# A two-layer encoder trunk on one core: start addresses of the split activations and blocks, 32-bit scores, and two block slots fewer

## The chip, the cores and the metric

The kernel runs on 1 core of a Trainium2 chip. The metric is device microseconds from start to end of one execution; a median over several runs stands for a kernel. The engines are TensorE (PE, with its weight loads shown apart as PEld), VectorE (DVE), ScalarE (ACT), GpSimd (POOL) and SyncE (SP), which issues the transfers.

## The reference: what is computed

Two sequences of 256 tokens (512 rows together), width 1024, go through two layers. Each layer is a mixer and a gated FFN with a three-tap convolution over tokens:

```python
h = rms_norm(x, norm_mix[i])
# layer 0: differential attention, 8 heads, two score maps per head, heads of 64
a = softmax(q0 k0) - lam * softmax(q1 k1);  o = a @ v;  o = rms_norm(o)
# layer 1: three dilated window groups of 8 heads of 64, joined by their log-sum-exp
# both layers: 4 heads of 64 of cross-attention into 256 memory tokens
x = x + concat([mixed, cross]) @ w_out
x = x + (silu(a) * b) @ w_down,   a, b = conv3(rms_norm(x) @ w_up)
```

q and k of every attention are normalised per head and, but for the cross-attention, rotated on 16 of their 64 elements.

## The kernel before

**Products.** A float32 operand of a large product is held as two parts, a high part rounded to the 32-bit form fp32r and a low part (the rest). `mm3` (L370 to L374) makes one product of three matmuls: high by high (L371), then the two mixed ones (L372, L373). In the trace a matmul's tiles are written out<-moving,stationary. In the QKV projections the activations `hh`, `hl` are stationary and the weights `wh`, `wl` move; in the FFN's up-projection the weights are stationary and `hh`, `hl` move; in the down-projection and the output projection the activations lie in block slots (`blk`) and are stationary.

**Storage.** `hh` and `hl` are [128, 8, 512] fp32r tiles. `blk` is a pool of 30 slots of 128 x 512 elements; a `Slots` object gives out the slot that comes free first. Slots hold gains and memory tokens as they land, q and k blocks, v, the split outputs of attention and the split FFN activations (20 slots in the first of the three FFN parts, 16 in the second, 8 in the third). Before the last FFN part of layer 0, `mem_tiles` loads and normalises the memory tokens of layer 1 into slots while the second part's are still held.

**Scores.** `qk_post` (L599) normalises, rotates and transposes q or k. `block_evac` (L572) then takes a block of two heads (64 partitions each) from its PSUM bank. For kind "-" one ACT instruction (L575) makes one float32 block. For kinds "q" and "k" two ACT instructions (L582) write the high parts of the two heads to two blocks, and two DVE instructions (L587) the low parts; for q the low part lies in the other 64 partitions of the same block, for k in a third block, and two more DVE copies (L594) repeat k's high part. So a matmul over 128 partitions (L833) gives high by high plus low by high, and one over 64 partitions (L835) adds high by low. Blocks of kind "-" are multiplied as plain float32 over 64 partitions (L840); there are two heads, on partitions 0 to 63 and 64 to 127. All scores over 256 keys are of the first sort (L833, L835); in layer 1 the two groups over 128 keys are of the second (L840). Each float32 matmul appears as two MATMUL records.

A score group is what `scores` (L827) issues for one tile of 128 tokens: two pieces of 256 keys in layer 0's mixer (4 head pairs x 4 tiles = 16 groups) and in the cross-attention (2 layers x 4 tiles = 8 groups), one piece of 256 and two of 128 in layer 1's mixer (16 groups).

**Order.** The order of all instructions is worked out while the kernel is built: generators run against a small model of the engines (`Sched`, with costs such as `c_act`, `c_dve`, `c_mm`), and whichever part is due next writes its instructions. Attention work is thus laid between the projections' matmuls. Weights come as 220 units of 512 KB through `raw` slots on SP's queue, are split by ACT (L348) and DVE (L350), and are held in 6 slots of `wh` and `wl`.

Of the kernel before, what the change touches and what calls it, by code (L numbers as in the profile page):

```python
# [21 lines left out]
NTOK = 512  # L22
# [5 lines left out]
LAM_INIT = 0.8 - 0.6 * math.exp(0.0)  # L28
BIG = 1e30
QS = -0.125  # L30
N_BLK, N_W = 30, 6
X0_U, X1_U = 1, 3
FIRST = [(0, 0), (1, 0), (0, 1), (1, 1), (2, 0), (2, 1), (0, 2), (1, 2), (2, 2), (3, 0), (3, 1), (3, 2), (0, 3), (1, 3), (2, 3), (3, 3)]
X_AT = (1, 2, 3)
# [5 lines left out]
class Event:  # L40
    def __init__(self, sched):
        self.s, self.t, self.waiters, self.val = sched, None, [], None
# [51 lines left out]
class Slots:  # L94


    def __init__(self, sched, pool, name, n, shape):
        self.s, self.pool, self.name, self.shape = sched, pool, name, shape
        self.free = [(0.0, i) for i in range(n)]
        self.waiters = deque()  # L100

    def get(self, dt=F32):
        if self.free:
            j = min(range(len(self.free)), key=lambda i: self.free[i])
            t, i = self.free.pop(j)
            if t > self.s.now:
                yield t
        else:
            e = self.s.event()
            self.waiters.append(e)  # L110
            yield e
            i = e.val
        v = self.pool.tile(self.shape, dt, tag=f"{self.name}{i}", bufs=1, name=f"{self.name}{i}")
        return Slot(self, i, v)

    def put(self, i, t):
        if self.waiters:
# [144 lines left out]
def trunk_kernel(ctx: ExitStack, tc: tile.TileContext, io: dict, out: bass.AP):  # L262
# [6 lines left out]
    small = ctx.enter_context(tc.tile_pool(name="small", bufs=6))  # L269
    psum = ctx.enter_context(tc.tile_pool(name="psum", bufs=1, space=bass.MemoryType.PSUM))  # L270

    def slots(name, n, shape=(128, 512)):
        return Slots(S, pool, name, n, list(shape))

    blk = slots("blk", N_BLK)
    e_s = slots("e", 3)
    eT_s = slots("eT", 3)
    on_s = slots("on", 1)
# [154 lines left out]
            tp.done(t)  # L433
        yield t

    hh = const.tile([128, KD, NTOK], F32R, name="hh")
    hl = const.tile([128, KD, NTOK], F32R, name="hl")

    def norm_h(t, gkey, permuted, x_ev, h_ev):

# [105 lines left out]
            if all((u, x) == (u, t) or FIRST.index((u, x)) < FIRST.index((u, t)) for x in range(NT)):  # L546
                ws[u][2](S.free["PE"])

    class QBlock:


        def __init__(self, a):
            self.a = a

        def done(self, t):
            for x in self.a:
                x.done(t)

    class KBlock:


        def __init__(self, a, lo):
            self.a, self.lo = a, lo

        def done(self, t):
            for x in self.a + [self.lo]:
                x.done(t)

    def half(h):
        return slice(64 * h, 64 * h + 64)  # L570

    def block_evac(kind, bufs, tp, g):  # L572

        if kind == "-":
            nc.scalar.activation(bufs[0].v, tp.v, AF.Copy, scale=g)  # L575
            t = S.op("ACT", c_act(512, 1))
            yield t
            tp.done(t)
            return bufs[0]
        for h in range(2):  # L580
            pr = half(h)
            nc.scalar.activation(bufs[h].v[pr], tp.v[pr], AF.Copy, scale=g[pr])  # L582
            yield S.op("ACT", c_act(512, 1))
        for h in range(2):
            pr, po = half(h), half(1 - h)
            lo = bufs[2].v[pr] if kind == "k" else bufs[h].v[po]
            nc.vector.scalar_tensor_tensor(lo, tp.v[pr], g[pr], bufs[h].v[pr].bitcast(F32), ALU.mult, ALU.subtract)  # L587
            t = S.op("DVE", c_dve(512, 1))
        tp.done(t)
        yield t  # L590
        if kind == "q":
            return QBlock(bufs)
        for h in range(2):
            nc.vector.tensor_copy(bufs[h].v[half(1 - h)], bufs[h].v[half(h)].bitcast(F32))  # L594
            t = S.op("DVE", c_dve(512, 0, True))
        yield t
        return KBlock(bufs[0:2], bufs[2])

    def qk_post(rope, gcol, kinds, ev):  # L599

        qns = [None] * 2
        evs = [S.event() for _ in range(NT)]
# [1 line left out]
        def post(t, ps, done):  # L604
# [37 lines left out]
            if t == NT - 1:  # L642
                for e in evs:
                    yield e
                dst = []
                for b in range(2):
                    bufs = []
                    for _ in range({"-": 1, "q": 2, "k": 3}[kinds[b]]):
                        d = yield from blk.get(F32 if kinds[b] == "-" else F32R)
                        bufs.append(d)  # L650
                    tp = yield from tp_s.get()
                    for x in range(NT):
                        src = qns[x // 2].val.v.rearrange("p (t c) -> p t c", t=2)
                        nc.tensor.transpose(tp.v[:, x * 128:x * 128 + 128], src[:, x % 2, b * 128:b * 128 + 128],  # L654
                                            ident)
                        te = S.op("PE", T_PE)
                    yield te
                    d = yield from block_evac(kinds[b], bufs, tp, gcol[b])
                    dst.append(d)
                for q in qns:  # L660
                    q.val.done(te)
                ev.set(S.now, dst)
# [164 lines left out]
    def scores(sc, parts):  # L827

        for c, q, tq, k, ks in parts:
            n = ks.stop - ks.start  # L830
            if isinstance(q, QBlock):
                for h in range(2):
                    nc.tensor.matmul(sc[h].v[:, c:c + n], q.a[h].v[:, tq], k.a[h].v[:, ks], start=True, stop=False)  # L833
                for h in range(2):
                    nc.tensor.matmul(sc[h].v[:, c:c + n], q.a[h].v[half(h), tq], k.lo.v[half(h), ks],  # L835
                                     start=False, stop=True)
                t = S.op("PE", 4 * c_mm(n))
            else:
                for h in range(2):
                    nc.tensor.matmul(sc[h].v[:, c:c + n], q.v[half(h), tq], k.v[half(h), ks], start=True, stop=True)  # L840
                    t = S.op("PE", c_mm(n, True))
        return t

    def take(slots_, ev):
# [536 lines left out]
    def main():  # L1381
        ev = S.event

        xq, mk, mv = ev(), ev(), ev()
        cross = [ev(), ev()]
        mT = [ev() for _ in range(NT)]
        halves = [qk_post(None, gc(G_XQ[0], G_XQ[0]), "qq", xq)]
        outs = []
        for p in range(4):
            q, k, v = ev(), ev(), ev()  # L1390
            halves += [qk_post(ropes["aq"], gc(G_AQ, G_AQ), "qq", q), qk_post(ropes["ak"], gc(G_AK, G_AK), "kk", k), v_post(v)]
            res = [ev(), ev()]
            outs.append(res)
            S.spawn(attn_a(q, k, v, res))
        yield from proj_first("a_w_in", halves[0:2], h0)
        S.spawn(mem_tiles(0, mT))
        yield from proj("a_w_in", halves[2:4])
        S.spawn(attn_cross(xq, mk, mv, False, cross))
        a_outs = {"c": cross, **{str(i): x for i, x in enumerate(outs)}}
        for st in A_STEPS:  # L1400
            if st[0] == "M":
                yield from mem_proj(0, mT, [qk_post(None, gc(G_XK[0], G_XK[0]), "kk", mk), v_post(mv)])
            elif st[0] == "P":
                yield from proj("a_w_in", [halves[1 + 3 * int(n) + "qkv".index(x)] for x, n in st[1:]])
            else:
                yield from out_proj("a_w_out", a_outs[st[1]], None)
        x1 = [ev() for _ in range(NT)]
        h1 = norm_all("f0", io["norm_ffn"][0], False, x1)
        yield from out_proj_last("a_w_out", [a_outs[x] for x in A_LAST], x1)
        x2 = [ev() for _ in range(NT)]  # L1410
        mT = [ev() for _ in range(NT)]
        xq, mk, mv = ev(), ev(), ev()
        h2 = norm_all("h1", io["norm_mix"][1], True, x2, mv)
        yield from ffn(0, h1, x2, mT, [qk_post(None, gc(G_XK[1], G_XK[1]), "kk", mk), v_post(mv)])

        cross = [ev(), ev()]
        halves = [qk_post(None, gc(G_XQ[1], G_XQ[1]), "qq", xq)]
        S.spawn(attn_cross(xq, mk, mv, True, cross))
        outs = []
        for p in range(4):  # L1420
            q01, q2k0, k12, v01 = ev(), ev(), ev(), ev()
            halves += [qk_post(ropes["b0"], gc(G_BQ[0], G_BQ[1]), "q-", q01), qk_post(ropes["b1"], gc(G_BQ[2], G_BK[0]), "-k", q2k0),
                       qk_post(ropes["b2"], gc(G_BK[1], G_BK[2]), "--", k12), v_post(v01)]
            if p % 2 == 0:
                v2 = ev()
                halves.append(v_post(v2))
            res = ev()
            outs.append(res)
            S.spawn(attn_b(q01, q2k0, k12, v01, v2, (p % 2) * 128, p % 2 == 1, res))
        for i in range(0, len(halves), 2):  # L1430
            yield from proj("b_w_in", halves[i:i + 2], h2 if i == 0 else None, True)
        yield from out_proj("b_w_out", outs[0:2], None)
        x3 = [ev() for _ in range(NT)]
        h3 = norm_all("f1", io["norm_ffn"][1], False, x3)
        yield from out_proj_last("b_w_out", [cross, outs[2:4]], x3)
        yield from ffn(1, h3, None)
# [70 lines left out]
```

## Time and profile before

| | |
|---|---|
| median of 3 runs | 1434.92 us (1434.71 to 1435.49) |
| the profiled execution, its own time | 1434.02 us |
| its span in the trace | 1432.2 us |
| PE busy | 1402.8 us, 98% of the span |
| PEld busy | 1171.2 us |
| DVE, ACT, POOL busy | 841.1, 644.5, 338.4 us |
| chain that ended last | PE 87%, POOL 5%, DVE 3% |

The span runs from the first to the last instruction; what lies around it is 1.8 us. A matmul's shown duration is its modelled stay in the array and overlaps the next one's, so how fast PE goes is read from the distance between starts, or from how many matmuls fit in a stretch, not from the duration.

### The profile page before, as it was taken

What the parts mean: (1) busy time and instruction counts of PE and PEld (TensorE: products, weight loads), DVE (VectorE), ACT (ScalarE), POOL (GpSimd) and SP (SyncE); (2) the same over time, 40 slices, a digit from 0 to 9 for tenths busy, and PEclk for the clock granted to TensorE, in tenths of its full rate; (3) what the DMA queues carried; (4) which work ended last, traced back from release to release, by engine and by line L of the source; (5) the groups of instructions that cost most, each with busy time, mean ns of one, the idle gap of its engine ahead of it and who ended that gap; (6) DMA issues with size and microseconds to landing.
All of it is one profiled execution on the core that took longest, in us unless ns stands there. A gap on an engine that the chain in (4) does not pass through costs nothing.

```text
span 1432.2 us, 19017 instructions
## 1 busy us (share of the span) xinstructions
PE 1402.8 (98%) x7168; PEld 1171.2 (82%) x7168; DVE 841.1 (59%) x1314; ACT 644.5 (45%) x1177; POOL 338.4 (24%) x652
## 2 busy tenths in 40 slices
PE   6999999999999999999999999999999999999999
PEld 4778888879888888878878888888889888888887
DVE  5687778886664356546666444444476663466353
ACT  5666656535443144344446434444554442243231
POOL 5836554121000000030154155545130000000000
PEclk9999999999999999999999999999999999999999
DMA  6431131122333333433231222212223333323321
GB/s 224 156 97 50 33 110 60 60 74 89 118 95 97 101 90 103 114 122 121 73 93 53 72 70 66 60 60 74 88 78 100 103 89 102 94 98 103 89 74 59
DMA packets 39260, 129.33 MB, mean 90 GB/s; under 512 B 4608, under 2 KB 5504, under 8 KB 39168
## 3 DMA queue, kind: packets, MB, share of 16 engines
q1 hardware_dynamic: 39168, 128.11, 28.9%
q8 instruction: 57, 0.93, 0.3%
q14 instruction: 35, 0.29, 0.1%
HBM read 126.00 MB, written 2.10 MB: 89 GB/s over the span
## 4 chain that ended last, share of the span: by engine, by line
PE 87%; POOL 5%; DVE 3%; issue 2%; DMA 1%; ACT 1%; SPq 0%; POOLq 0%; DVEq 0%; ACTq 0%
PE acc L371 17%; PE acc L373 17%; PE acc L372 17%; PE sc L373 7%; PE sc L371 7%; PE sc L372 7%; PE tp L755 2%; POOL rstd L620 2%; PE o L1038 2%; PE sc L835 1%; PE sc L833 1%; PE tp L654 1%; PE tp L415 1%; PE o L371 1%; PE o L372 1%
## 5 line engine op out<-in xcount | busy, mean ns | idle before, releaser
L350 DVE TENSOR_TENSOR wl<-raw,wh 128x1024 fp32r<-128x1024 f32 x220 | 273.4, 1246 | 239.2 <-ACT wh L348 238.4
L348 ACT CAST wh<-raw 128x1024 fp32r<-128x1024 f32 x220 | 231.9, 1055 | 357.6 <-PE sc L372 182.3
L371 PE MATMUL acc<-wh,hh 128*128 128x512 f32 (+1 forms) x536 | 217.0, 405 | 0.6 <-ACT hh L428 0.6
L373 PE MATMUL acc<-wh,hl 128*128 128x512 f32 (+1 forms) x536 | 203.5, 380 | 0.0
L372 PE MATMUL acc<-wl,hh 128*128 128x512 f32 (+1 forms) x536 | 203.1, 379 | 0.0
L371 PE MATMUL acc<-wh,blk 128*128 128x512 f32 x368 | 148.9, 405 | 0.0
L372 PE MATMUL acc<-wl,blk 128*128 128x512 f32 x368 | 143.6, 390 | 0.0
L373 PE MATMUL acc<-wh,blk 128*128 128x512 f32 x368 | 143.5, 390 | 0.0
L371 PE MATMUL acc<-hh,wh 128*128 128x512 f32 (+1 forms) x384 | 143.1, 373 | 0.0
L371 PE MATMUL sc<-hh,wh 128*128 128x512 f32 (+1 forms) x384 | 142.9, 372 | 0.0
L373 PE MATMUL acc<-hh,wl 128*128 128x512 f32 (+1 forms) x384 | 142.6, 371 | 0.0
L373 PE MATMUL sc<-hh,wl 128*128 128x512 f32 (+1 forms) x384 | 142.6, 371 | 0.0
L372 PE MATMUL acc<-hl,wh 128*128 128x512 f32 (+1 forms) x384 | 142.6, 371 | 0.0
L372 PE MATMUL sc<-hl,wh 128*128 128x512 f32 (+1 forms) x384 | 142.6, 371 | 0.0
L373 PEld LDWEIGHTS acc<-wh,hl 128*128 128x128 f32 x536 | 101.1, 189 | 19.9 <-DVE hl L430 0.3
L371 PEld LDWEIGHTS acc<-wh,hh 128*128 128x128 f32 x536 | 101.8, 190 | 16.7 <-ACT hh L428 1.0
L372 PEld LDWEIGHTS acc<-wl,hh 128*128 128x128 f32 x536 | 101.7, 190 | 13.9 <-DVE wl L350 0.5
L386 POOL TENSOR_SCALAR s<-ss 128x1 f32<-128x1 f32 x24 | 11.4, 477 | 427.7 <-ACT qn L381 422.1
L620 POOL TENSOR_TENSOR rstd<-ss,mhalf 128x4 f32<-128x4 f32 x96 | 106.2, 1107 | 8.0
L373 PEld LDWEIGHTS acc<-hh,wl 128*128 128x128 f32 x384 | 72.3, 188 | 12.5
L372 PEld LDWEIGHTS acc<-hl,wh 128*128 128x128 f32 x384 | 72.3, 188 | 12.5
L373 PEld LDWEIGHTS sc<-hh,wl 128*128 128x128 f32 x384 | 72.3, 188 | 12.5
(152 smaller groups left out, 2486.7 us busy)
## 6 DMA issues: line engine op xcount, KB each, us to landing
raw<-w SPq DMA_DIRECT2D x220, 512.0 KB, 3.6
blk<-mem SPq DMA_DIRECT2D x16, 256.0 KB, 6.6
y<-X SPq DMA_DIRECT2D x8, 256.0 KB, 2.0
X<-x SPq DMA_DIRECT2D x3, 512.0 KB, 9.0
blk<-norm_mix SPq DMA_DIRECT2D x4, 256.0 KB, 6.3
blk<-norm_mem SPq DMA_DIRECT2D x4, 256.0 KB, 6.0
blk<-norm_ffn SPq DMA_DIRECT2D x4, 256.0 KB, 5.3
X<-x SPq DMA_DIRECT2D x2, 256.0 KB, 3.0
```

Of the source, the lines that this page charges most:

```text
L348: nc.scalar.copy(hi.v, r.v)
L350: nc.vector.tensor_tensor(lo.v, r.v, hi.v.bitcast(F32), ALU.subtract)
L371: nc.tensor.matmul(out_, ah, bh, start=start, stop=False)
L372: nc.tensor.matmul(out_, ah, bl, start=False, stop=False)
L373: nc.tensor.matmul(out_, al, bh, start=False, stop=stop)
L415: nc.tensor.transpose(tp.v[:, k * 128:k * 128 + 128], h[j].v[:, k * 128:k * 128 + 128], ident_)
L620: nc.gpsimd.tensor_tensor(rstd, ss, mhalf[:, 0:4], ALU.pow)
L654: nc.tensor.transpose(tp.v[:, x * 128:x * 128 + 128], src[:, x % 2, b * 128:b * 128 + 128], ident)
L755: nc.tensor.transpose(tp.v[:, i * 128:i * 128 + 128], e.v[:, i * 128:i * 128 + 128], ident)
L833: nc.tensor.matmul(sc[h].v[:, c:c + n], q.a[h].v[:, tq], k.a[h].v[:, ks], start=True, stop=False)
L835: nc.tensor.matmul(sc[h].v[:, c:c + n], q.a[h].v[half(h), tq], k.lo.v[half(h), ks], start=False, stop=True)
L1038: nc.tensor.matmul(o[:, t, h, :], eT.v[:, i * 128:i * 128 + 128], vt[s].v[:, c:c + 64], start=(i == 0), stop=(i == 3))
```

## The change

Four edits. (1) `hh` and `hl` get 16 elements more and begin 4 and 12 elements (16 and 48 bytes) into their tiles. (2) Each block slot gets 16 elements more, and slot i begins i mod 16 elements (0, 4 ... 60 bytes) into its tile. (3) All blocks of q and k are plain float32: `block_evac`, `QBlock` and `KBlock` are gone, every block is taken from PSUM by one ACT instruction, and every score is a float32 matmul over 64 partitions; the model's cost of such a pair of matmuls is counted once for the two heads. (4) 28 block slots in place of 30.

```diff
-N_BLK, N_W = 30, 6
+N_BLK, N_W = 28, 6
...
+        at = i * self.phase % 16
+        shape = [self.shape[0], self.shape[1] + (16 if self.phase else 0)]
+        v = self.pool.tile(shape, dt, tag=f"{self.name}{i}", bufs=1, name=f"{self.name}{i}")
+        return Slot(self, i, v[:, at:at + self.shape[1]])
...
-    blk = slots("blk", N_BLK)
+    blk = slots("blk", N_BLK, phase=1)
...
-    hh = const.tile([128, KD, NTOK], F32R, name="hh")
-    hl = const.tile([128, KD, NTOK], F32R, name="hl")
+    hht = const.tile([128, KD * NTOK + 16], F32R, name="hh")
+    hlt = const.tile([128, KD * NTOK + 16], F32R, name="hl")
+    hh = hht[:, 4:4 + KD * NTOK].rearrange("p (k t) -> p k t", k=KD)
+    hl = hlt[:, 12:12 + KD * NTOK].rearrange("p (k t) -> p k t", k=KD)
...
-                    bufs = []
-                    for _ in range({"-": 1, "q": 2, "k": 3}[kinds[b]]):
-                        d = yield from blk.get(F32 if kinds[b] == "-" else F32R)
-                        bufs.append(d)
+                    d = yield from blk.get()
+                    dst.append(d)
...
-                    d = yield from block_evac(kinds[b], bufs, tp, gcol[b])
-                    dst.append(d)
+                    nc.scalar.activation(d.v, tp.v, AF.Copy, scale=gcol[b])
+                    tp.done(S.op("ACT", c_act(512, 1)))
+                    yield S.free["ACT"] + S.LAT
...
-            if isinstance(q, QBlock):
-                for h in range(2):
-                    nc.tensor.matmul(sc[h].v[:, c:c + n], q.a[h].v[:, tq], k.a[h].v[:, ks], start=True, stop=False)
-                for h in range(2):
-                    nc.tensor.matmul(sc[h].v[:, c:c + n], q.a[h].v[half(h), tq], k.lo.v[half(h), ks],
-                                     start=False, stop=True)
-                t = S.op("PE", 4 * c_mm(n))
-            else:
-                for h in range(2):
-                    nc.tensor.matmul(sc[h].v[:, c:c + n], q.v[half(h), tq], k.v[half(h), ks], start=True, stop=True)
-                    t = S.op("PE", c_mm(n, True))
+            for h in range(2):
+                nc.tensor.matmul(sc[h].v[:, c:c + n], q.v[half(h), tq], k.v[half(h), ks], start=True, stop=True)
+            t = S.op("PE", c_mm(n, True))
```

The calls of `qk_post` lose their kinds ("qq", "kk", "q-", "-k", "--").

## Rows read from the trace of the kernel before

**Rows 1.** The page, busy time of the engines, share of the span, instructions.

```profile
PE 1402.8 (98%) x7168; PEld 1171.2 (82%) x7168; DVE 841.1 (59%) x1314; ACT 644.5 (45%) x1177; POOL 338.4 (24%) x652
```

**Rows 2.** Waits of PE over the span: engine, line, releaser: us, times, longest.

```profile
PE tp L415 <- DMA ident<-c_ident: 8.2, 1, 8.2
PE tp L415 <- DVE qn L403: 5.2, 7, 1.4
PE tp L654 <- POOL qn L639: 3.7, 3, 1.9
...
PE tp L415 <- DVE blk L587: 0.6, 1, 0.6
...
PE tp L654 <- DVE blk L587: 0.5, 1, 0.5
```

**Rows 3.** Windows: an attention stretch and an FFN stretch; busy us and counts.

```profile
100.00:200.00 100.00, 100.00 (x558) 82.06 (x557) 78.83 (x171) 61.55 (x163) 52.07 (x116) 1.00 0.21 61
...
400.00:500.00 100.00, 100.00 (x443) 82.84 (x442) 47.42 (x55) 29.87 (x36) 0.00 (x0) 1.00 0.32 96
```

**Rows 4.** Timeline of PE at 332 us: start, us, engine, line, tiles, shapes.

```profile
332.01 0.28 PE L373 MATMUL sc<-hh,wl 128*128 128x256 f32 x1
...
332.37 0.28 PE L373 MATMUL sc<-hh,wl 128*128 128x256 f32 x1
```

**Rows 5.** Timeline of PE, one score group of layer 0 and its successor.

```profile
126.00 0.40 PE L833 MATMUL sc<-blk,blk 128*128 128x256 f32 x2
...
126.63 0.50 PE L833 MATMUL sc<-blk,blk 128*128 128x256 f32 x2
...
127.38 0.50 PE L371 MATMUL acc<-wh,hh 128*128 128x512 f32 x1
```

**Rows 6.** Timeline of PE, a layer 1 group; its L840 also cut short.

```profile
800.59 0.40 PE L833 MATMUL sc<-blk,blk 128*128 128x256 f32 x2
800.91 0.38 PE L835 MATMUL sc<-blk,blk 64*128 64x256 f32 x2
801.13 0.61 PE L840 MATMUL sc<-blk,blk 64*128 64x128 f32 x8
801.67 0.50 PE L371 MATMUL acc<-wh,hh 128*128 128x512 f32 x1
...
801.13 0.27 PE L840 MATMUL sc<-blk,blk 64*128 64x128 f32 x2
```

**Rows 7.** Groups by line and shape, ACT and DVE: the blocks taken from PSUM.

```profile
L582 ACT ACTIVATE blk<-tp,gcols 64x512 fp32r<-64x512 f32 x64 | 43.6, 684 | 27.9 <-PE tp L654 27.3
L575 ACT ACTIVATE blk<-tp,gcols 128x512 f32<-128x512 f32 x16 | 11.1, 693 | 7.9 <-PE tp L654 7.8
L587 DVE SCALAR_TENSOR_TENSOR blk<-tp,gcols,blk 64x512 fp32r<-64x512 f32 x64 | 47.9, 749 | 23.0 <-ACT blk L582 22.2
L594 DVE CAST blk<-blk 64x512 fp32r<-64x512 f32 x32 | 13.5, 423 | 0.7
```

**Rows 8.** Groups by line: products that move `hh`, and loads from `hh` and `blk`.

```profile
L371 PE MATMUL acc<-hh,wh 128*128 128x512 f32 (+1 forms) x384 | 143.1, 373 | 0.0
L371 PEld LDWEIGHTS acc<-wh,hh 128*128 128x128 f32 x536 | 101.8, 190 | 16.7 <-ACT hh L428 1.0
L371 PEld LDWEIGHTS acc<-wh,blk 128*128 128x128 f32 x368 | 69.2, 188 | 12.6
L371 PEld LDWEIGHTS sc<-wh,blk 128*128 128x128 f32 x104 | 19.5, 188 | 4.0
L371 PEld LDWEIGHTS o<-wh,blk 128*128 128x128 f32 x72 | 13.5, 188 | 2.8
```

**Rows 9.** Groups by line and shape, DVE: output begins 4 bytes later, or not.

```profile
L1156 DVE SCALAR_TENSOR_TENSOR eT<-sc,convT,eT 128x510 f32<-128x510 f32 x44 | 32.9, 749 | 2.8 <-ACT eT L1151 2.8
L1158 DVE SCALAR_TENSOR_TENSOR eT<-sc,convT,eT 128x510 f32<-128x510 f32 x44 | 32.9, 749 | 1.6
```

**Rows 10.** Transfers into block slots: count, KB each, us to landing.

```profile
blk<-mem SPq DMA_DIRECT2D x16, 256.0 KB, 6.6
```

More of the change, by code (lines that the diff above doesn't have):

```diff
@@ L94, with __init__ @@
 class Slots:
-    def __init__(self, sched, pool, name, n, shape):
-        self.s, self.pool, self.name, self.shape = sched, pool, name, shape
+    def __init__(self, sched, pool, name, n, shape, phase=0):
+        self.s, self.pool, self.name, self.shape, self.phase = sched, pool, name, shape, phase
         self.free = [(0.0, i) for i in range(n)]
@@ L112, in get @@
             i = e.val
-        v = self.pool.tile(self.shape, dt, tag=f"{self.name}{i}", bufs=1, name=f"{self.name}{i}")
-        return Slot(self, i, v)
+        at = i * self.phase % 16
+        shape = [self.shape[0], self.shape[1] + (16 if self.phase else 0)]
+        v = self.pool.tile(shape, dt, tag=f"{self.name}{i}", bufs=1, name=f"{self.name}{i}")
+        return Slot(self, i, v[:, at:at + self.shape[1]])
     def put(self, i, t):
@@ L270, in trunk_kernel, with slots @@
     psum = ctx.enter_context(tc.tile_pool(name="psum", bufs=1, space=bass.MemoryType.PSUM))
-    def slots(name, n, shape=(128, 512)):
-        return Slots(S, pool, name, n, list(shape))
-    blk = slots("blk", N_BLK)
+    def slots(name, n, shape=(128, 512), phase=0):
+        return Slots(S, pool, name, n, list(shape), phase)
+    blk = slots("blk", N_BLK, phase=1)
     e_s = slots("e", 3)
@@ L547, in proj_first, with qk_post @@
                 ws[u][2](S.free["PE"])
[L549 to L567, printed above, removed]
     def half(h):
         return slice(64 * h, 64 * h + 64)
[L572 to L579, printed above, removed]
-        for h in range(2):
-            pr = half(h)
-            nc.scalar.activation(bufs[h].v[pr], tp.v[pr], AF.Copy, scale=g[pr])
-            yield S.op("ACT", c_act(512, 1))
-        for h in range(2):
[L585 to L592, printed above, removed]
-        for h in range(2):
[L594 to L599, printed above, removed]
+    def qk_post(rope, gcol, ev):
         qns = [None] * 2
@@ L830, in scores @@
             n = ks.stop - ks.start
-            if isinstance(q, QBlock):
-                for h in range(2):
-                    nc.tensor.matmul(sc[h].v[:, c:c + n], q.a[h].v[:, tq], k.a[h].v[:, ks], start=True, stop=False)
-                for h in range(2):
-                    nc.tensor.matmul(sc[h].v[:, c:c + n], q.a[h].v[half(h), tq], k.lo.v[half(h), ks],
-                                     start=False, stop=True)
-                t = S.op("PE", 4 * c_mm(n))
-            else:
-                for h in range(2):
-                    nc.tensor.matmul(sc[h].v[:, c:c + n], q.v[half(h), tq], k.v[half(h), ks], start=True, stop=True)
-                    t = S.op("PE", c_mm(n, True))
+            for h in range(2):
+                nc.tensor.matmul(sc[h].v[:, c:c + n], q.v[half(h), tq], k.v[half(h), ks], start=True, stop=True)
+            t = S.op("PE", c_mm(n, True))
         return t
@@ L1386, in main @@
         mT = [ev() for _ in range(NT)]
-        halves = [qk_post(None, gc(G_XQ[0], G_XQ[0]), "qq", xq)]
+        halves = [qk_post(None, gc(G_XQ[0], G_XQ[0]), xq)]
         outs = []
@@ L1390, in main @@
             q, k, v = ev(), ev(), ev()
-            halves += [qk_post(ropes["aq"], gc(G_AQ, G_AQ), "qq", q), qk_post(ropes["ak"], gc(G_AK, G_AK), "kk", k), v_post(v)]
+            halves += [qk_post(ropes["aq"], gc(G_AQ, G_AQ), q), qk_post(ropes["ak"], gc(G_AK, G_AK), k), v_post(v)]
             res = [ev(), ev()]
@@ L1401, in main @@
             if st[0] == "M":
-                yield from mem_proj(0, mT, [qk_post(None, gc(G_XK[0], G_XK[0]), "kk", mk), v_post(mv)])
+                yield from mem_proj(0, mT, [qk_post(None, gc(G_XK[0], G_XK[0]), mk), v_post(mv)])
             elif st[0] == "P":
@@ L1413, in main @@
         h2 = norm_all("h1", io["norm_mix"][1], True, x2, mv)
-        yield from ffn(0, h1, x2, mT, [qk_post(None, gc(G_XK[1], G_XK[1]), "kk", mk), v_post(mv)])
+        yield from ffn(0, h1, x2, mT, [qk_post(None, gc(G_XK[1], G_XK[1]), mk), v_post(mv)])
         cross = [ev(), ev()]
-        halves = [qk_post(None, gc(G_XQ[1], G_XQ[1]), "qq", xq)]
+        halves = [qk_post(None, gc(G_XQ[1], G_XQ[1]), xq)]
         S.spawn(attn_cross(xq, mk, mv, True, cross))
@@ L1421, in main @@
             q01, q2k0, k12, v01 = ev(), ev(), ev(), ev()
-            halves += [qk_post(ropes["b0"], gc(G_BQ[0], G_BQ[1]), "q-", q01), qk_post(ropes["b1"], gc(G_BQ[2], G_BK[0]), "-k", q2k0),
-                       qk_post(ropes["b2"], gc(G_BK[1], G_BK[2]), "--", k12), v_post(v01)]
+            halves += [qk_post(ropes["b0"], gc(G_BQ[0], G_BQ[1]), q01), qk_post(ropes["b1"], gc(G_BQ[2], G_BK[0]), q2k0),
+                       qk_post(ropes["b2"], gc(G_BK[1], G_BK[2]), k12), v_post(v01)]
             if p % 2 == 0:
```

## The prediction

> **What bounds the kernel now.** I read the busy times first, then what PE waited for, then two windows, and last the timeline around the scores. PE is busy for 1402.8 of 1432.2 us [rows 1]. Its waits are short: the longest is 8.2 us for the identity matrix at the very start, and after that the rows name waits of a few us for normalised rows [rows 2]. An FFN stretch and an attention stretch both show PE busy for 100.00 of 100 us at a granted clock of 1.00, which is 2.4 GHz, while DVE is at 79% and ACT at 62% at most [rows 3]. So PE sets the time, and what counts is how many us of PE's stream an edit adds or takes.
>
> How fast does PE go? 443 matmuls start in 100 us of the FFN [rows 3], 0.226 us each, where 512 columns at 2.4 GHz are 0.2133. Matmuls of 256 columns start 0.36 us apart for three steps [rows 4], 0.120 each, where the columns are 0.1067. Both pay 12 to 13 ns beyond their columns, per instruction and not per column. This sum is what the start addresses could act on.
>
> **The scores.** A group of two pieces of 256 keys takes from 126.00 to 127.38, 1.38 us [rows 5]. There are 24 such groups, 33.1 us. A layer 1 group takes from 800.59 to 801.67, 1.08 us [rows 6]; 16 groups are 17.3 us. What will they take as float32 over 64 partitions? The trace has that form already, at 128 columns (L840). Eight records span 0.61 us and the first two 0.27 [rows 6]: three further steps take 0.34 us, and as each step brings two records, records run in pairs, 0.113 us a pair. That fits the two heads lying on different halves of the array. A pair of 256 columns is bounded by two passes over the columns at 2.4 GHz, 0.213, and by twice the row, 0.227; I take 0.22. A piece of 256 keys has two heads of two records, two pairs, 0.44 us.
>
> Going into and out of the 64-partition form costs something, and the same rows show it. The last pair starts 0.34 us after 801.13, at 801.47, and its successor at 801.67: 0.20, which is 0.09 more than a step. On the way in, the two L833 take 0.32 us [rows 6] where two matmuls of 256 columns take 0.24 [rows 4], 0.08 more. The group before goes in and out once per piece; the new one goes in and out once in all. So a layer 0 group becomes 4 x 0.22 + 0.09 + 0.08 = 1.05 us, 0.33 less, and 24 of them give 7.9 us. A layer 1 group becomes 2 x 0.22 + 4 x 0.113 + 0.17 = 1.06, 0.02 less, 0.3 us for 16. Together 8.2 us less on PE, between 7.2 and 9.2 with the two bounds of the pair.
>
> **The evacuation of q and k.** Gone are 64 ACT instructions of 684 ns, 64 DVE of 749 and 32 DVE of 423; 32 more ACT instructions of 693 ns come [rows 7]. ACT loses 43.6 - 22.2 = 21.4 us, DVE 61.4. Neither is the bound [rows 3], so I count only the PE waits that name L587, 0.6 and 0.5 us [rows 2], as 1 us. At least nothing is gained, and at most the waits of rows 2 other than the first, some 10 us; the 1 us is nearest to what names these lines. The weight splits that queue behind these instructions on ACT and DVE come earlier too; no wait of rows 2 names them, so that is worth nothing.
>
> **The start addresses.** In the kernel before, every tile and every slice that PE reads begins at a multiple of 64 bytes, so no row has the price, and it has to be bounded. On the moving side there are six groups like the one shown of 384 matmuls that move `hh` or `hl`, 2304 in all [rows 8]. On the stationary side there are 3 x 536 loads from `hh` and `hl` and 3 x (368 + 104 + 72) = 1632 from blocks [rows 8]. If the 13 ns per instruction vanished on all 5544 of these, 74 us would go; if they doubled, 74 us would come; on the moving side alone it is 31 us either way. The nearest row for a shifted start is DVE's: writing 4 bytes further along, the same instruction takes 749 ns, as it does unshifted [rows 9]. That the extra is alike for 512 and 256 columns also looks like a cost of changing from one matmul to the next rather than of reading. I take zero and keep both ends. A longer load would be covered: it lasts 188 to 190 ns [rows 8] under a step of 226, so it has 36 ns to spare.
>
> DVE and ACT instructions on shifted blocks I cost at nothing: by rows 9 they take no longer, and if they did, the waits of PE that name them are those of rows 2. Against this stands the Trainium skill, Vector Engine (DVE) Microarchitecture Reference, section 5.2, Measured stream behaviour on trn2: a port keeps its rate for runs of adjacent words from an 8-byte boundary, and for pairs from an odd word it gives 1.30 against 1.054 ns per column. By that an odd slot would slow a 0.75 us instruction by some 0.13 us (estimate), which changes the sum by nothing while DVE has 20% idle; rows 9 do not show it for one long run.
>
> Transfers into shifted slots, of 6.6 us to landing [rows 10], feed gains and memory tokens. Except at the start no wait of rows 2 names a transfer, and there the identity is last. Zero; a landing later by 1 us would cost at most that at the start.
>
> **28 slots.** Attention needs fewer slots than before: two for a q of two blocks in place of four, two for a k in place of six. The FFN parts hold 20, 16 and 8. Tight is only the loading of layer 1's memory tokens, with 12 free slots in place of 14 while 16 are held. Slots come free as the down-projection goes on, so I take zero; the cover is that down-projection, and without it a wait of about one landing, 6.6 us, would show.
>
> **The sum.** 8.2 + 1 = 9.2 us less. The profiled execution took 1434.02 us, so 1424.8; the median shown is 0.90 above that execution, which makes **1425.7 us**. With the bounds of the pair (7.2 to 9.2) and of the waits (0 to 10) this case spans 1416 to 1428. About 0.2% (2.9 us) is what a measurement of this kernel can tell from no change.
>
> **The rivals.**
>
> *Shifted moving reads cost more* (slower). If a moving operand at 16 or 48 bytes needs one fetch more than one at a multiple of 64, each of the 2304 matmuls pays. Half of the 13 ns, 6.7, gives 15.4 us and 1441; the full 13.3 gives 1456. The scores' gain is used up from 9.2 us / 2304 = 4 ns per matmul. For it: 512 and 256 columns pay the same extra [rows 3, 4], as they would if each instruction began with a fetch that its columns don't hide. Against it: the unshifted and the shifted instruction of DVE take the same time [rows 9]. Chance 0.18.
>
> *Shifted operands cost less.* If the 13 ns come from the moving and the stationary read beginning alike, shifting one against the other removes part of them: 31 us for the moving side, 1395, or 74 us for all, 1352. For it: every operand shown has the same extra, and all begin alike. Against it: an extra that is a change-over stays. The Trainium skill, TensorE: Matmul & The Clock Gate, Part 2, speaks against it too: the two reads have ports of their own and do not slow one another; by that rule the time stays at the sum's. Chance 0.14.
>
> *Loads from blocks become the bound* (slower). A load of 188 ns would have to pass 226. If loads from the odd slots, half of 1632, took half as long again, 282 ns, that is 56 x 816 = 46 us more, 1472. Chance 0.04.
>
> *The gain is eaten.* PE reaches its next transposes 0.33 us earlier per group and waits there for softmax, or waits for one of the 28 slots; the time stays at about 1434. For it: chains over POOL and DVE end some of PE's waits [rows 2]. Against it: those waits are a few us in all, and DVE gets 61 us of relief. Chance 0.07.
>
> **The numbers.** 0.57 for the forecast. Faster: 0.57 + 0.14 = 0.71. Same: 0.07 and 0.02 of the first rival where its price is near 4 ns, 0.09. Slower: 0.16 + 0.04 = 0.20. The range takes in the forecast's span, the first rival to 8 ns a matmul and the second to some 21 us: 1404 to 1444. Left out are 0.09 of the second, 0.07 of the first and the third's 0.04.
>
> **What would show it.** The scores: no L833 or L835 line; layer 0 groups of about 1.05 us from first score to successor. The addresses: still 443 matmuls per 100 us in the FFN; some 430 there would be the first rival, over 450 the second. If the projections and down-projections slow down while the up-projections do not, it is the loads. The evacuation: ACT about 21 and DVE about 61 us less busy. A wait of PE for memory tokens in the FFN of layer 0 would speak for the slots. The prediction is wrong if the FFN's count per 100 us moves by more than about 1%.

## The result and the profile after

The change makes the kernel slower: 1451.96 us median (1450.87 to 1452.53, 4 runs) beside 1435.03 for the kernel before on the same chip (4 runs), a ratio of 1.0119 with a 95% interval of 1.0105 to 1.0134. The forecast was 1425.7 with a range up to 1444; the sign is wrong, and the time lies outside the range.

The page of the changed kernel, busy times (beside [rows 1]):

```profile
PE 1422.1 (98%) x7168; PEld 1162.7 (80%) x7168; DVE 784.0 (54%) x1218; ACT 621.0 (43%) x1145; POOL 335.6 (23%) x652
```

Its span is 1450.2 us, 18.0 more. DVE has 57 us less to do and ACT 23.5 (about 61 and 21 were forecast), and PE is busy 19.3 us longer with the same 7168 matmuls. Is it a new wait? The waits of PE, the longest of them (beside [rows 2]):

```profile
PE tp L417 <- DMA ident<-c_ident: 8.6, 1, 8.6
PE tp L417 <- DVE qn L405: 5.8, 9, 1.2
PE tp L417 <- DVE hl L432: 4.6, 6, 1.8
PE tp L609 <- POOL qn L596: 3.6, 3, 1.6
```

No. These are the old ones, within a few us, and no new wait for a slot or a landing has come in. The windows of the changed kernel (beside [rows 3]; columns PE, PEld, DVE, ACT, POOL, granted clock, DMA share, GB/s):

```profile
100.00:200.00 100.00, 100.00 (x554) 80.22 (x553) 61.03 (x134) 56.00 (x146) 53.79 (x118) 1.00 0.21 64
400.00:500.00 100.00, 100.00 (x431) 80.52 (x430) 44.87 (x51) 29.40 (x35) 0.00 (x0) 1.00 0.31 92
```

431 matmuls start in 100 us of the FFN instead of 443, at the same granted clock of 1.00 and with PE busy all the time. Each step has grown. The timeline of PE at 400 us shows it one by one (start, us, engine, line, tiles, shapes):

```profile
400.01 0.40 PE L373 MATMUL sc<-hh,wh 128*128 128x512 f32 x1
400.25 0.39 PE L374 MATMUL sc<-hl,wh 128*128 128x512 f32 x1
400.48 0.39 PE L375 MATMUL sc<-hh,wl 128*128 128x512 f32 x1
400.71 0.40 PE L373 MATMUL acc<-hh,wh 128*128 128x512 f32 x1
400.95 0.39 PE L374 MATMUL acc<-hl,wh 128*128 128x512 f32 x1
401.18 0.39 PE L375 MATMUL acc<-hh,wl 128*128 128x512 f32 x1
401.41 0.40 PE L373 MATMUL acc<-hh,wh 128*128 128x512 f32 x1
```

Two triples take 1.40 us, 0.2333 a step. In the kernel before, two triples took 1.36, 0.2267 a step:

```profile
400.15 0.39 PE L371 MATMUL acc<-hh,wh 128*128 128x512 f32 x1
...
401.51 0.39 PE L371 MATMUL sc<-hh,wh 128*128 128x512 f32 x1
```

The loads have not grown with the steps. Three groups of the weight loads of the changed kernel (beside [rows 8]):

```profile
L374 PEld LDWEIGHTS acc<-hl,wh 128*128 128x128 f32 x384 | 72.3, 188 | 14.3
L375 PEld LDWEIGHTS acc<-hh,wl 128*128 128x128 f32 x384 | 71.9, 187 | 15.3
L373 PEld LDWEIGHTS acc<-wh,blk 128*128 128x128 f32 x368 | 69.3, 188 | 15.3 <-issue 1.7
```

Summing the distances between the starts of successive matmuls over the whole of both traces, by kind of matmul, splits the 18.0 us (a step is the distance to the next start; 0.1 us lies behind the last start):

| us | before | after | difference |
|---|---|---|---|
| steps of 512-column fp32r matmuls (4963, 4969) | 1164.6 | 1189.5 | +24.9 |
| steps of 256-column fp32r matmuls (574, 573) | 71.3 | 70.3 | -0.9 |
| score records (384) | 51.5 | 42.8 | -8.7 |
| the step just ahead of each of the 40 score groups | 7.2 | 10.8 | +3.6 |
| transposes, the rest, start of the first matmul | 133.8 | 132.8 | -1.0 |

The six steps of 512 columns that the change has more there are 1.4 us of the first line. So there are two findings: 512-column steps that are 23.5 / 4969, some 5 ns, longer, which is more than the whole loss, and a score gain of which part is lost in the step that leads into each group.

### The profile page after: what moved, and what is told of

Same layout as the page of the kernel before. It is cut to its first block, busy times and chain, and to the rows that moved or that the text cites. A ratio compares the mean times of both kernels' runs of the same rounds, so it can differ in the third digit from the quotient of the medians.

```text
span 1450.2 us, 18857 instructions
## 1 busy us (share of the span) xinstructions
PE 1422.1 (98%) x7168; PEld 1162.7 (80%) x7168; DVE 784.0 (54%) x1218; ACT 621.0 (43%) x1145; POOL 335.6 (23%) x652
## 3 DMA queue, kind: packets, MB, share of 16 engines
HBM read 126.00 MB, written 2.10 MB: 88 GB/s over the span
## 4 chain that ended last, share of the span: by engine, by line
PE 89%; POOL 4%; DMA 2%; DVE 2%; issue 2%; ACT 1%; SPq 0%; POOLq 0%; DVEq 0%
PE acc L373 18%; PE acc L375 17%; PE acc L374 17%; PE sc L373 7%; PE sc L375 7%; PE sc L374 7%; PE sc L788 3%; PE tp L711 2%; PE o L986 2%; PE tp L609 1%; POOL rstd L577 1%; PE o L375 1%; PE o L374 1%; PE o L373 1%; PE tp L417 1%
## 5 line engine op out<-in xcount | busy, mean ns | idle before, releaser
L373 PE MATMUL acc<-wh,blk 128*128 128x512 f32 x368 | 150.4, 409 | 0.0
L375 PE MATMUL acc<-wh,blk 128*128 128x512 f32 x368 | 145.4, 395 | 0.0
L571 DVE TENSOR_REDUCE ss<-sq 128x4 f32<-128x256 f32 x96 | 39.8, 415 | 90.9 <-ACT sq L568 90.5
```

Of the source, the lines that this page charges most:

```text
L373: nc.tensor.matmul(out_, ah, bh, start=start, stop=False)
L375: nc.tensor.matmul(out_, al, bh, start=False, stop=stop)
L571: nc.vector.tensor_reduce(ss, sq.v[:, 0:256].rearrange("p (a d) -> p a d", d=64), AX.X, ALU.add)
```

## The experiments

All kernels below have the plain scores. In the built programs, `hh`, `hl`, weights and blocks of the kernel before all start at multiples of 2048 bytes: their lengths are multiples of that, and a spacer of 64 elements ahead of `X` puts the first there. The change ends this twice over: `hh`, `hl` and most blocks no longer start at multiples of 64 bytes (below, they start "inside 64 bytes"), and the 64 bytes added to each of these tiles displace what is laid behind it by multiples of 64.

The table gives for each kernel the median, the ratio to the kernel before on the same chip, and the matmuls of PE in two windows: 505 to 575 us, an up-projection (`hh`, `hl` move, weights are loaded), and 445 to 485 us, a down-projection (weights move, blocks are loaded).

| kernel | us | ratio, 95% interval | up, 70 us | down, 40 us |
|---|---|---|---|---|
| before | 1434.85 to 1435.21 | | 311 | 178 |
| the change | 1451.96 | 1.0119 [1.0105, 1.0134] | 301 | 173 |
| scores | 1430.94 | 0.997 [0.9961, 0.998] | 311 | 179 |
| slots28 | 1430.67 | 0.9972 [0.996, 0.9984] | 310 | 178 |
| pad64 | 1454.16 | 1.0141 [1.0125, 1.0156] | 301 | 175 |
| hshift | 1440.87 | 1.0042 [1.0025, 1.0059] | 306 | 178 |
| blkphase | 1439.77 | 1.003 [1.0017, 1.0043] | 311 | 174 |
| pad256 | 1431.62 | 0.997 [0.9961, 0.998] | 310 | 178 |
| h128 | 1447.27 | 1.0084 [1.0067, 1.0101] | 302 | 179 |
| all128 | 1430.32 | 0.997 [0.9957, 0.9983] | 310 | 178 |
| starts | 1446.92 | 1.0083 [1.0068, 1.0098] | 306 | 174 |

### Scores alone, and the slots

**scores** is the change without its start addresses and with 30 slots:

```diff
-N_BLK, N_W = 28, 6
+N_BLK, N_W = 30, 6
...
-    blk = slots("blk", N_BLK, phase=1)
+    blk = slots("blk", N_BLK)
...
-    hht = const.tile([128, KD * NTOK + 16], F32R, name="hh")
...
+    hh = const.tile([128, KD, NTOK], F32R, name="hh")
...
```

(`hl` likewise.)

> The kernel before with the plain 32-bit scores alone: 30 slots, every tile where it was, all at multiples of 2048 bytes. If the loss comes from where operands lie, the FFN keeps 443 matmuls per 100 us and the whole gains what the scores' rows of the changed kernel give: some 5 us with the way in and out, so 1427 to 1430. If the loss comes from the new score form or the order of the work around it, this is slower than 1435.

**slots28** is the same with `N_BLK` 28.

> The plain scores with 28 slots in place of 30, every tile at a multiple of 2048 bytes. If two slots cost nothing, as forecast: equal to the scores alone (1430.9, within 2 us). If slots are short: more, with waits of PE in layer 0's FFN near the memory tokens.

Plain scores alone gain 4.0 us, and two slots fewer add or take nothing (0.3 us between the two kernels, their ranges lie over one another). Why 4 and not 8.2? The timeline of PE in slots28, a score group of layer 0, its predecessors and its successor:

```profile
92.51 0.39 PE L374 MATMUL acc<-wl,blk 128*128 128x512 f32 x1
92.74 0.39 PE L375 MATMUL acc<-wh,blk 128*128 128x512 f32 x1
93.06 1.13 PE L786 MATMUL sc<-blk,blk 64*128 64x256 f32 x8
94.12 0.44 PE L709 MATMUL tp<-ident,e 128*128 128x128 f32 x2
```

The group takes 1.06 us, from 93.06 to 94.12, which is the 1.05 of the forecast. But the matmul ahead of it starts at 92.74 and holds the group up for 0.32 us, where a step is 0.23. The kernel before, ahead of the group of [rows 5], which starts at 126.00:

```profile
125.77 0.39 PE L373 MATMUL acc<-wh,hl 128*128 128x512 f32 x1
```

There it is 0.23. The way into a run of 64-partition matmuls is paid in the step before its first start, and a count from first start to successor does not see it. Over the 40 groups these steps come to 10.8 us instead of 7.2, and as more of them are now short transposes (10 of 40, 6 before), what they cost beyond ordinary steps (0.227 us for 512 columns, 0.120 for 256, 0.105 for the others) went from -0.45 to 3.84, some 4.3 us more. The score records gain 8.7 us here too; 8.7 less 4.3 is 4.4 us, and the spans differ by 1432.2 - 1428.0 = 4.2.

### Which starts cost

**pad64** keeps the longer tiles of the change and begins every operand at byte 0 of its tile, so that all start at multiples of 64:

```diff
-        at = i * self.phase % 16
+        at = 0
...
-    hh = hht[:, 4:4 + KD * NTOK].rearrange("p (k t) -> p k t", k=KD)
-    hl = hlt[:, 12:12 + KD * NTOK].rearrange("p (k t) -> p k t", k=KD)
+    hh = hht[:, 0:KD * NTOK].rearrange("p (k t) -> p k t", k=KD)
+    hl = hlt[:, 0:KD * NTOK].rearrange("p (k t) -> p k t", k=KD)
```

> The changed kernel with the same longer tiles, but every tile read from its start, so that all starts are multiples of 64 bytes, only no longer of 2048. If starts inside 64 bytes cost the time, this is as fast as the scores alone (1427 to 1430, 443 matmuls per 100 us of FFN). If it is the displacement of the tiles against each other, this is nearly as slow as the change: 1445 to 1455, 430 to 436 per 100 us.

**hshift** keeps every tile at a multiple of 2048 and only reads `hh` and `hl` from bytes 16 and 48 (28 slots, blocks neither longer nor shifted). Against the change, besides the blocks:

```diff
-    hht = const.tile([128, KD * NTOK + 16], F32R, name="hh")
-    hlt = const.tile([128, KD * NTOK + 16], F32R, name="hl")
+    hht = const.tile([128, KD * NTOK + 512], F32R, name="hh")
+    hlt = const.tile([128, KD * NTOK + 512], F32R, name="hl")
```

> Plain scores, 28 slots, all tiles at multiples of 2048 bytes, and only hh and hl read from 16 and 48 bytes on. If each moving read that begins off pays, the up-projections fall to about 430 per 100 us, the down-projections stay at 443, and the whole is some 13 to 17 us above the scores alone. If only the blocks matter, it is equal to the scores alone.

**blkphase** moves the blocks alone (`hh` and `hl` as in slots28). They are laid last, so that nothing else moves, and keep the change's longer slots: they lie 2112 bytes apart, slot i beginning 4 x (i mod 16) bytes into its tile. So a block is off in two ways, by its start inside 64 bytes and by the multiples of 64 that the longer slots add up to:

```diff
+    for y in (e_s, eT_s, on_s, qn_s, sq_s, raw_s, wh_s, wl_s):
+        for _, i in y.free:
+            pool.tile(y.shape, F32, tag=f"{y.name}{i}", bufs=1, name=f"{y.name}{i}")
```

> Plain scores, 28 slots, hh, hl, weights and all else at multiples of 2048 bytes; only the block slots lie last, 2112 bytes apart, and begin at 0, 4 ... 60 bytes more. If weight loads from shifted blocks cost, the down-projections fall from 443 to about 430 per 100 us and the up-projections stay at 443: some 1632 x 6 ns = 10 us above the scores alone. If loads stay covered, it is equal to the scores alone.

Windows of slots28, then of pad64, of hshift and of blkphase (busy time and matmuls of PE, granted clock, DMA share, GB/s):

```profile
445.00:485.00 40.00, 40.00 (x178) 1.00 0.32 93
505.00:575.00 70.00, 70.00 (x310) 1.00 0.33 98
```

```profile
445.00:485.00 40.00, 40.00 (x175) 1.00 0.33 98
505.00:575.00 70.00, 70.00 (x301) 1.00 0.33 98
```

```profile
445.00:485.00 40.00, 40.00 (x178) 1.00 0.33 103
505.00:575.00 70.00, 70.00 (x306) 1.00 0.31 97
```

```profile
445.00:485.00 40.00, 40.00 (x174) 1.00 0.31 93
505.00:575.00 70.00, 70.00 (x311) 1.00 0.32 96
```

hshift slows the up-projection and leaves the down-projection alone; blkphase does the reverse, by reads that only feed weight loads. So both sides cost, each in its own stretch: 10.2 us more than slots28 (13 to 17 were expected) and 9.1 (10 expected). hshift shows that starts inside 64 bytes cost something by themselves; blkphase does not, since its slots are displaced as well. And pad64 loses more than either, 23.5 us, with no start inside 64 bytes at all. So starts inside 64 bytes can't be the only cause. What pad64 has is tiles displaced against one another by multiples of 64.

### Bare matmuls

**phases** and **phases2** leave the trunk out and copy the input to the output. They run rows of 512- or 256-column fp32r matmuls into one PSUM tile, one placement to a row, the weights loaded anew for each matmul (shortened: `s` and `m` set where the two operands begin, and `s` goes back and forth between two places 2048 bytes apart). Each of them was run once:

```python
for k in range(REP):
    mm(acc[:, 0:n], stat[:, s:s + 128], move[:, m:m + n], start=(k == 0), stop=(k == REP - 1))
```

> No trunk at all: the input is copied to the output, and 85 rows of 40 fp32r matmuls run back to back, each row with its own start of the moving operand (a) and of the stationary one (b), in bytes behind a multiple of 2048. If it is the place of the two reads against each other that counts, the distance of two starts depends on a - b: 0.2267 us at 0 and at multiples of 2048, 0.224 to 0.240 elsewhere, the same where both are shifted alike. If the start of each operand by itself counts (a fetch more for a read that is not aligned), rows with both shifted alike are as slow as or slower than those with one shifted, and b alone does nothing as loads are covered.

> No trunk: the input is copied to the output, and 66 rows of 42 fp32r matmuls run, with starts of the moving and the stationary reads laid out in grids of 16 and of 64 bytes and in the orders of the FFN's triples. By the distance modulo 256 alone, every row of the 64-byte grid with a = b takes 0.2267 and those 64, 128, 192 apart about 0.2333, 0.2324, 0.2289; the same starts inside 64 bytes take 0.2333 even where both are alike. The triple of the changed kernel's up-projection gives about 0.233 and that of pad64 0.234, that of before 0.2267.

Below, a placement is written moving start/weight start, in bytes behind a multiple of 2048. The timeline of PE in phases, one row a placement, of 40 matmuls: L156 is 0/0, L157 0/64, L158 0/128, L159 0/192, L160 0/256:

```profile
21.35 9.23 PE L156 MATMUL acc<-move,stat 128*128 128x512 f32 x40
30.42 9.49 PE L157 MATMUL acc<-move,stat 128*128 128x512 f32 x40
39.75 9.46 PE L158 MATMUL acc<-move,stat 128*128 128x512 f32 x40
49.05 9.32 PE L159 MATMUL acc<-move,stat 128*128 128x512 f32 x40
58.21 9.25 PE L160 MATMUL acc<-move,stat 128*128 128x512 f32 x40
67.29 9.49 PE L161 MATMUL acc<-move,stat 128*128 128x512 f32 x40
```

From start to start, 9.07, 9.33, 9.30, 9.16 and 9.08 us for 40: the weights' place alone, with no trunk beside it, changes the step. Leaving out the first five and last two distances of each row, it settles at 226.7 ns at 0, 233.3 at 64, 232.4 at 128, 228.9 at 192 and 226.7 again at 256, and so on to 1984 with a period of 256 bytes; at 4096 to 24576 it is 226.7. Now both sides shifted, in phases2 (42 to a row): L177 is 64/0, L178 64/64, L179 64/128:

```profile
215.83 9.78 PE L177 MATMUL acc<-move,stat 128*128 128x512 f32 x42
225.45 9.69 PE L178 MATMUL acc<-move,stat 128*128 128x512 f32 x42
234.98 9.96 PE L179 MATMUL acc<-move,stat 128*128 128x512 f32 x42
244.78 9.93 PE L180 MATMUL acc<-move,stat 128*128 128x512 f32 x42
```

9.62, 9.53, 9.80: settled, 229.0, 226.7 and 233.3. 64/64, 128/128 and 192/192 all go at 226.7. For starts at multiples of 64, it is not a start off 256 bytes that costs, but that the two reads do not start alike modulo 256. The direction counts: 64/0 goes like 0/192, not like 0/64. Triples placed like those of the kernel before settle at 227.4, two like those of the changed kernel at 235.6 and 233.4, and two like pad64's at 232.0 and 234.3.

The Trainium skill (TensorE: Matmul & The Clock Gate, Part 2) says that "Loading the next tile's weights doesn't steal SBUF read bandwidth from the running matmul"; these rows differ from it for this kind of matmul, by 6.6 ns a step, and the measurement decides.

### Displacement in the kernel

If displacement is the cause, pads of 256 bytes cost nothing. **pad256** is pad64 with these (and 26 slots, so that it fits):

```diff
-        shape = [self.shape[0], self.shape[1] + (16 if self.phase else 0)]
+        shape = [self.shape[0], self.shape[1] + (64 if self.phase else 0)]
...
-    hht = const.tile([128, KD * NTOK + 16], F32R, name="hh")
-    hlt = const.tile([128, KD * NTOK + 16], F32R, name="hl")
+    hht = const.tile([128, KD * NTOK + 64], F32R, name="hh")
+    hlt = const.tile([128, KD * NTOK + 64], F32R, name="hl")
```

> As pad64, but with 256 bytes of pad for each of hh, hl and the block slots in place of 64 (26 slots, for room), all read from the start of their tiles. Tiles are again displaced against each other and off the multiples of 2048, but all by multiples of 256. If what counts is the distance of the two reads modulo 256, as the row of phases says, it is as fast as the scores alone: 443 per 100 us in the FFN and 1429 to 1433. If tiles have to begin at multiples of 2048, it is as slow as pad64: 1450 to 1456.

It is as fast as scores alone. **h128** moves `hh` and `hl` by 128 bytes against all else, and **all128** moves everything by 128 together; both are slots28 but for these lines:

```diff
-    hh = const.tile([128, KD, NTOK], F32R, name="hh")
-    hl = const.tile([128, KD, NTOK], F32R, name="hl")
+    hht = const.tile([128, KD * NTOK + 512], F32R, name="hh")
+    hlt = const.tile([128, KD * NTOK + 512], F32R, name="hl")
+    hh = hht[:, 32:32 + KD * NTOK].rearrange("p (k t) -> p k t", k=KD)
+    hl = hlt[:, 32:32 + KD * NTOK].rearrange("p (k t) -> p k t", k=KD)
```

```diff
-    const.tile([128, 64], F32, name="spacer")
+    const.tile([128, 96], F32, name="spacer")
```

> Plain scores and 28 slots, every tile at a multiple of 2048 bytes, and only hh and hl begin 128 bytes into their tiles (a multiple of 64, and of 128, but not of 256). Theory (PE's step depends on how far the moving read and the weight load lie from one another modulo 256 bytes): the 2304 matmuls that move hh or hl and the 1608 that load their weights from them go from 226.7 to about 232.4 ns, the pace of the bare matmuls at a displacement of 128; 3912 x 5.7 ns = 22 us more than with 28 slots alone, about 1453, and some 430 matmuls per 100 us in the up-projection, 443 still in the down-projection, which reads neither. Rival (only starts inside 64 bytes and odd pads cost, a multiple of 128 doesn't): 1430.7.

> Plain scores and 28 slots, and the spacer ahead of x is 128 bytes longer, so that every later tile (hh, hl, weights, blocks) begins 128 bytes behind a multiple of 2048. Nothing is displaced against anything else. Theory (displacement of the two reads against one another): as with 28 slots alone, 1430.7, 443 matmuls per 100 us in the FFN. Rival (a start off a multiple of 256 costs by itself, on either side): at least as slow as with hh and hl alone so placed, 1453 or more, and 430 per 100 us in the up-projection and the down-projection.

Windows of h128, then of all128:

```profile
445.00:485.00 40.00, 40.00 (x179) 1.00 0.33 100
505.00:575.00 70.00, 70.00 (x302) 1.00 0.32 98
```

```profile
445.00:485.00 40.00, 40.00 (x178) 1.00 0.32 98
505.00:575.00 70.00, 70.00 (x310) 1.00 0.32 98
```

The same 128 bytes cost 17 us when one side moves and nothing when both do. h128 was expected at 1453 and came out at 1447.3: 534 of the 3912 matmuls in that forecast lie between others of 256 columns, whose step went down by 1 ns instead. The 1914 steps of 512 columns that move `hh` or `hl` went from 226.7 to 233.3 and the 1156 that load from them from 228.3 to 232.5: 12.6 + 4.9 - 0.5 = 17.0.

**starts** has the starts of the change inside 64 bytes and takes the displacing pads away from `hh` and `hl` only: it is blkphase, whose slots stay 2112 bytes apart, with `hh` and `hl` in tiles 256 bytes longer, read from bytes 16 and 48.

> The change's own starts without its displacing pads: hh and hl begin 16 and 48 bytes into tiles padded by 256 bytes, slot i begins 4 x (i mod 16) bytes into its tile, and the blocks lie last, so that weights and hh, hl are a multiple of 256 bytes apart but for the 16 and 48. Theory: the starts inside 64 bytes cost about what they cost one by one, 10.2 us for hh and hl and 9.1 us for the blocks over the 1430.7 of 28 slots alone: 1450, with some 435 per 100 us in the up-projection and 430 in the down-projection. Rival (without the pads the starts interact and cancel, or the pads are what loses): below 1441.

It loses 16.2 us over slots28 (some 19 were expected); its windows hold 306 and 174 matmuls, as hshift's and blkphase's do. The pads alone (pad64) lose 23.5 and the change, which has those pads and the starts, 21.3. Pads and starts don't add: once the reads are displaced, the starts inside 64 bytes bring no further loss here. How much of the loss in blkphase and starts comes from the blocks' starts and how much from the 64 bytes between their slots, no run parts; pad64, with the longer slots and no shifted start, holds 175 matmuls in the down-projection's window, nearly the same as their 174.

**phases3** asks whether the place alone sets the pace.

> Bare matmuls of 512 columns in fp32r, 42 to a row, eight placements (moving start/weight start in bytes behind a multiple of 2048: 0/0, 0/64, 0/128, 0/192, 0/16, 16/0, 16/16, 256/0), each run once after each of the others. The trunk is left out and the input copied to the output. Theory (placement alone sets the pace): each placement shows the same settled step in all its seven rows, 226.7 ns at 0/0 and 256/0, 233.3 at 0/64, 232.4 at 0/128. Rival (what ran before also counts): 0/192, which showed 228.9 ns in one run and 233.3 in another, and 0/16, which showed 233.3 and 226.7, take one or the other by their predecessor, while 0/0 and 256/0 always come back to 226.7.

Two rows of phases3 (42 to a row) at 0/16, each with its successor: L163, which follows 256/0, and L175, which follows 16/16:

```profile
80.19 9.68 PE L163 MATMUL acc<-move,stat 128*128 128x512 f32 x42
89.72 9.68 PE L164 MATMUL acc<-move,stat 128*128 128x512 f32 x42
...
195.61 9.96 PE L175 MATMUL acc<-move,stat 128*128 128x512 f32 x42
205.41 9.83 PE L176 MATMUL acc<-move,stat 128*128 128x512 f32 x42
```

9.53 and 9.80 us for the same placement: 0/16 settles at 226.7 behind five of its seven predecessors and at 233.3 behind 0/64 and 16/16. The others hardly care (0/64 233.3 in all seven, 0/128 232.4, once 233.2, 0/192 228.8 to 228.9, though 233.3 in phases2, 16/0 231.6 to 231.8, 16/16 229.9 to 231.1), and 0/0 and 256/0 come back to between 226.7 and 226.9 behind every one. So what ran before counts too where the reads are displaced or begin inside 64 bytes, and being alike is no safe rule there (16/16, and 48/48 with 233.3 in phases2, but 32/32 with 226.7). Two reads alike modulo 256 bytes and at multiples of 64 always settled at 226.7 to 227.4.

## Why the prediction was wrong

**The step that failed** is "I take zero and keep both ends", the price of the start addresses. Measured, the 512-column steps grew by 23.5 us, from 0.2267 to 0.2333 in the FFN's triples, and scores, evacuation and slots without the addresses run 21.3 us faster than the change (slots28). Three reasons stood behind the zero, and each failed in its own way. "A longer load would be covered": the loads did stay at 187 to 190 ns, but the step from one matmul to the next grows with the place that the weights are loaded from (phases, 0/64), so that the 36 ns to spare cover nothing of it. "The nearest row is DVE's" [rows 9]: it shows one engine reading by itself, and the cost lies between two reads of PE. And "a cost of changing from one matmul to the next rather than of reading": the bare matmuls show that the time beyond the columns hangs on where the operands lie, 2 to 10 ns more than the 13 for 512 columns and up to 6.7 less for 256.

**What was overlooked.** The text treated the edit as a shift inside 64 bytes. The 64 bytes of padding looked harmless, since every tile still starts at a multiple of 64 but for the stated shift; they alone lose as much as the change (pad64). That the kernel before had all its operands at one place modulo 256 bytes stood in its tile sizes and its spacer.

**The rivals.** *Shifted moving reads cost more* had the sign and, with "Half of the 13 ns, 6.7", the size of a step: 431 matmuls per 100 us is its mark, and 2.7% fewer than 443 is past the 1% that the prediction had named as the sign of being wrong. A moving start off a multiple of 64 does cost (hshift: 306 matmuls instead of 310 in the up-projection's window), but this is not what the change lost by: pad64 loses 23.5 us with every moving start at a multiple of 64, and by this rival would have lost nothing. The stationary side pays as well (blkphase: 174 instead of 178 in the down-projection). That its step comes near the measured one is luck. *Loads from blocks become the bound* fell: no load grew. *Shifted operands cost less* is true for 256 columns alone (-0.9 us). *The gain is eaten* fell for waits and slots.

**The scores.** Groups of 1.05 and 1.06 us were forecast and are 1.064 and 1.077 on average in slots28; the records gain 8.7 us where 8.2 were forecast. Mis-sized is the way in, counted once as "0.08". It has two parts: the matmul ahead of the first 64-partition start is held up, and the first pair itself takes 0.10 more than the next one (0.320 and 0.216). The 0.08 of [rows 6] is of the first sort, as its 0.32 ends where L835 starts; in the new groups that part lies ahead of the group, some 0.1 behind a matmul of 512 columns and more or less as much behind transposes, 4.3 us over 40 groups, and the first pair's 0.10 stood nowhere in the sum. That the groups came out as forecast is luck: one part stood in for the other. Plain scores are worth 4.0 to 4.5 us.

**The rest.** The evacuation took 23.5 us off ACT and 57 off DVE, near the forecast, and gained PE nothing that shows beside the scores: 8.7 - 4.3 = 4.4 us accounts for all of the 4.2 by which slots28 is shorter. No run has one without the other, so this is argued from the sum. DVE and ACT pay nothing for shifted blocks, as taken: they are busy for 784.0 and 621.0 us, 783.6 and 622.2 in slots28, and L432, which writes 44 split blocks on DVE, takes 686 ns in both kernels, so that the 0.13 us estimated for an odd slot don't show. The slots are zero, as taken. In the terms of the sum: scores, evacuation and slots ended at 1430.7 (slots28) instead of 1425.7, and the addresses add 21.3, which makes 1452.0.

**What stays open.** That displaced reads meet in the same part of a memory that is laid out in turns of 256 bytes would fit the period, but no run shows it. Nor is it known why 0/16 settles in one of two ways, what the blocks' starts inside 64 bytes cost by themselves, or whether matmuls in another format or without a load for each show any of this.

## What to carry to other kernels

Before lengthening a tile or moving an operand, look where the moving operand and the next weights lie modulo 256 bytes: in this fp32r kernel keeping them alike, at multiples of 64, is worth some 5 ns in each of 5000 matmuls, and pads in multiples of 256 bytes cost nothing here (pad256). Price a change of matmul form from the start of the matmul ahead of it to the second one after, since a group that is timed from its first start hides the way in. Of this change the plain scores are worth keeping, alone or with fewer slots (0.997 of the time before).

## What the runs showed of the hardware

In the bare fp32r rows, with a weight load for each matmul, the pace hangs on the distance of the two reads modulo 256 bytes: 226.7 ns for 512 columns when alike at multiples of 64 (up to 227.4 where the first steps of the row still differ), 228.9 to 233.3 at other multiples of 64, and from 226.7 to 236.7 with one start inside 64 bytes or both (4/0 and 16/32 are the slowest, 28/0 and 60/0 among the free ones). A triple that mixes both, 64/12, 64/12 and 64/16, settled at 240.3. For 256 columns the displaced rows are the faster ones. The timeline of phases2, L217 with 0/64 and L218 with 0/192, 42 matmuls of 256 columns to a row:

```profile
605.34 4.94 PE L217 MATMUL acc<-move,stat 128*128 128x256 f32 x42
610.12 4.92 PE L218 MATMUL acc<-move,stat 128*128 128x256 f32 x42
614.88 4.93 PE L219 MATMUL acc<-move,stat 128*128 128x256 f32 x42
```

4.78 and 4.76 us for 42; settled, 113.3 ns a step, where 0/0 and 0/256 have 120.0 and 0/128 118.5. Half of the 13 ns beyond the columns is gone there, so for 256 columns that much of it was not a fixed cost; no placement tried went below 226.7 for 512.
